# Ten units of a gated feed-forward stage read the moving operand of their matmuls in ten other column orders

## The chip, the cores and the metric

The kernel runs on one core of one Trainium2 chip. The metric is the device time of one execution in microseconds, from the runs of the whole program; details come from one profiled execution.

## The reference: what is computed

One layer of a decoder on 256 tokens of width 2048, all in float32. Three sub-layers, each behind an RMSNorm: a gated feed-forward network with 5632 hidden columns (its result is halved), a mixer of two groups of attention heads, and a second gated network like the first.

```python
def swiglu(x, w_gate, w_up, w_down):
    return (jax.nn.silu(x @ w_gate) * (x @ w_up)) @ w_down

h = h + 0.5 * swiglu(rms_norm(h, norm_ffn1_g[l]), ffn1_w_gate[l], ffn1_w_up[l], ffn1_w_down[l])
...
h = h + o @ w_out[l]
h = h + 0.5 * swiglu(rms_norm(h, norm_ffn2_g[l]), ffn2_w_gate[l], ffn2_w_up[l], ffn2_w_down[l])
```

The 5632 hidden columns of the first network are independent of each other up to the last product, which sums over them. If the columns of gate and up are computed in another order, the result is the same as long as the rows of `w_down` stand in that order too.

## The kernel before

**Products.** Every large product of float32 matrices is made of three matmuls: each operand is split into a high part in float32r and a low part (what the high part left), and `mm3` (L400 to L402) adds high by high, high by low and low by high into one PSUM bank. The stationary operand is a 128 x 128 piece of the activations, the moving operand is a 128 x 512 piece of the weights, and 512 columns of PSUM are written.

**Units.** `ffn` (one call for each feed-forward network) walks the hidden columns in NB = 11 blocks of 512. A *unit* b makes gate and up of a block for all 256 tokens, from eight tiles of weights of 128 x 2048 (four pieces of 512 columns each: two of gate, two of up). A tile is used in one of two ways, which a string names for each unit. "D" is plain: eight products, from the four pieces and two halves of the tokens. "S" is a scheme with seven products, for which VectorE forms sums of the pieces (tile `sums`), so that seven pieces of 512 columns are used. Unit 0 has eight D, unit 1 four D and four S, unit 2 two D and six S, units 3 to 10 one D and seven S: 64, 60, 58 and 57 products.

**Down.** Behind unit b + 1 come the products of block b with its `w_down` rows (`down`, 32 products): the gated block is turned into rows by eight transposes (`turned`, L602) into the tile `hT`, which is the stationary operand there; the moving operand is again 512 columns of weights. The order is in PLAN:

```python
PLAN = [("U", 0)] + [x for b in range(1, NB) for x in (("U", b), ("D", (b - 1,)))][:-1] + [("D", (NB - 2, NB - 1))]
```

**Weights on their way.** A tile of weights comes by one DMA on SP's queue into `raw` (`rawx`, `rawy` are further buffers of the same kind), ScalarE casts it to the high part (`whi`, `whix`, `whiy`), and VectorE subtracts for the low part (`wlo`, `wlox`, `wloy`, L464). The sums of the S scheme are cast and split in the same way. All tiles are 2048 columns wide, and a piece is a run of 512 of them.

**Order.** `Task` objects carry each instruction's engine, cost and needs; `arrange` simulates them with a table of costs and writes out the order of all five engines. In `group` the products of one tile are made, each by `product`, whose `run` calls `mm3` with the views of one piece: `w[1]()` gives the high and the low part's view. `product` and `group` know nothing of the unit's number in the kernel before.

**Arrays.** `_arrays` lays out the inputs on the host ahead of the launch; `by_two` arranges `w_down` for the loads.

Of the kernel before, what the change touches and what calls it, by code (L numbers as in the profile page):

```python
# [36 lines left out]
NB = FF // 512  # L37
# [12 lines left out]
F2_ORDER = [(0, "rawy", F32)] + [(2, "whiy", F32R), (3, "wloy", F32R)] * FREE2 + [(1, "sums", F32)] * NSUM  # L50
F2_ORDER += [(2, "whiy", F32R)] * (NHI - 2 - FREE2) + [(3, "wloy", F32R)] * (NLO - 2 - FREE2) + [(0, "rawy", F32)] * (NRAW - 3)
PAD = 48


C_ID, C_INVF, C_ONE, C_TRI, C_MSK = 0, 128, 160, 288, 416
# [218 lines left out]
def hybrid_layer(ctx: ExitStack, tc: tile.TileContext, a: dict, out: bass.AP):  # L274
# [124 lines left out]
    def mm3(o, shi, slo, mhi, mlo, start, stop, seeded=False):  # L399
        nc.tensor.matmul(o, lhsT=shi, rhs=mhi, start=start, stop=False, skip_group_check=seeded)  # L400
        nc.tensor.matmul(o, lhsT=shi, rhs=mlo, start=False, stop=False, skip_group_check=seeded)  # L401
        return nc.tensor.matmul(o, lhsT=slo, rhs=mhi, start=False, stop=stop, skip_group_check=seeded)  # L402
# [29 lines left out]
    def ffn(pool, u, wgu, wd, slots, banks, rstd, held=None, first=None, lead=None, done=None, out=None):  # L432
# [26 lines left out]
        def bank_of(b):  # L459
            return banks[b["first"].got["bank"][0]]  # L460
# [82 lines left out]
            new = [(ld, -30), (c, 0), (a, 0), (l, 0)] + [(t, 3) for t in (ca, b0, b, cb, ls)]  # L543
            return new, w, {2: [("hi", c), ("lo", l)], 6: [("hi", ca), ("lo", ls)]}

        def product(held, key, stat, w, need):

            t = task("pe", 0.681, None, list(need) + w[0], lag=0.25)
            b = held.setdefault(key, {"first": t})
            if "seed" in b and "last" not in b:  # L550
                t.need.append(b["first"])
            if b["first"] is t:
                t.take = {"bank": 1}
            b["last"] = t

            def run():
                t.made = mm3(bank_of(b), *stat(), *w[1](), start=b["first"] is t, stop=b["last"] is t, seeded="seed" in b)

            t.run = run
            main.append(t)  # L560
            return t

        def group(kind, src, held, stat, need, form=None, pieces=1, last=False, behind=None):

            new, w, free = seven(src) if kind == "S" else added_low(src) if kind == "L" else whole(src, pieces, behind)
            n0 = len(main)
            if kind == "S":
                for i, (key, k, t) in enumerate((
                    ("Q0", 0, 0), ((0, 0), 1, 0), ((0, 1), "f", 0), ("Q1", "f", 3),
                    ("Q3", "f", 2), ("Q2", "f", 1), ((1, 0), 1, 1),  # L570
                )):
                    sh = (lambda t=t: form[1](t)) if k == "f" else (lambda k=k, t=t: stat(k, t))
                    x = product(held, key, sh, w[i], form[0] if k == "f" else need(k))
                    x.give = free.get(i, [])
            else:
                order = [(i, t) for i in range(4) for t in range(NT)]
                if last:
                    order.sort(key=lambda it: it[1])
                for i, t in order:
                    k = (0, 1, 1, 0)[i]  # L580
                    x = product(held, (t, i // 2), lambda k=k, t=t: stat(k, t), w[i], need(k))
                x.give = list(free[3])
            for t, d in new:
                t.due = n0 + d
            return n0
# [65 lines left out]
        forms = {}  # L651
# [44 lines left out]
        def unit(b):  # L696

            kinds, ns = units[b], count[b]
            pair = {"S": iter(sorted(seven_of[:ns])), "D": iter(sorted(seven_of[ns:]))}
            held, hs, sq3 = {}, [], []  # L700
            for n, kind in enumerate(kinds):
                p = next(pair["D" if kind == "L" else kind])
                if b == 0 and first is not None:
                    first[0](p, task, ready)
                if kind == "S" and p not in forms:
                    fresh[p] = len(main)
                    form_of(p, used.get(p, []) + [x for k in (2 * p, 2 * p + 1) for x in ready.get(k, ())], len(main) - 4)
                n0 = group(
                    kind, wgu[b][p], held, lambda k, t, p=p: halves(u(2 * p + k), t), lambda k, p=p: ready.get(2 * p + k, ()),
                    forms.get(p) if kind == "S" else None, (4, 2)[p] if b == 0 and first is not None and p < 2 else 1, n == len(kinds) - 1,  # L710
                )
                used[p] = [main[-1]]
                if b == 0 and first is not None:
                    hs.append(first[1](p, task))
# [11 lines left out]
            if ns:  # L726
                q = task("act", cast(512), None, [held["Q0"]["last"]], due, take={"s": 1, "sq": 2}, give=[("bank", held["Q0"]["first"])])
                x, y = lambda: sq_tile(q, 0), lambda: sq_tile(q, 1)
# [16 lines left out]
                v = [step(up[0], (0, 1), y, ALU.add, [d2], due + 1, False), step(up[1], (1, 1), x, ALU.add, [d4], due + 5, False)]  # L745
            ends = []
            for t in range(NT):
                src = (lambda t=t: s_tile()[:, t, :]) if ns else (lambda t=t: bank_of(R(t, 0)))
                a = task("act", 0.63, lambda t=t, src=src: nc.scalar.activation(
                    s_tile()[:, t, :], src(), AF.Silu, scale=rms[0][:, t : t + 1]  # L750
                ), [g[t] if ns else R(t, 0)["last"]] + rm_need, due + 9 if ns else due + 2 * t, take={"s": 1} if not ns and t == 0 else ())
                if t == 0:
                    a0 = a
                if not ns:
                    a.give.append(("bank", R(t, 0)["first"]))
                src = lambda t=t: bank_of(R(t, 1))
                f = task("dve", 0.66, lambda t=t, src=src: stt(
                    out=s_tile()[:, t, :], in0=src(), scalar=half_rms()[:, t : t + 1], in1=s_tile()[:, t, :], op0=ALU.mult, op1=ALU.mult,
                ), [a, v[t] if ns else R(t, 1)["last"]], due + 9 if ns else due + 2 * t, lag=1.5, psum=True)
# [646 lines left out]
def _arrays(x, positions, norm_ffn1_g, ffn1_w_gate, ffn1_w_up, ffn1_w_down, norm_mix_g, w_in, b_forget,  # L1406
            fox_q_norm_g, fox_k_norm_g, swa_q_norm_g, swa_k_norm_g, swa_sinks, out_norm_fox_g, out_norm_swa_g,
            w_out, norm_ffn2_g, ffn2_w_gate, ffn2_w_up, ffn2_w_down):
    f32 = np.float32
    d = {}  # L1410

    def blocks(w, rows, cols):

        n, m = w.shape
        w = w.reshape(n // P // rows, rows, P, m // cols, cols).transpose(3, 0, 2, 1, 4)
        return w.reshape(m // cols, n // P // rows, P, rows * cols)

    def cols(w):
        return blocks(w, 2, 512)

    def twos(w0, w1):

        x = np.stack([cols(w0).reshape(-1, w0.shape[0] // (2 * P), P, 2, 512), cols(w1).reshape(-1, w1.shape[0] // (2 * P), P, 2, 512)])
        x = np.stack([x[0, ..., 0, :], x[0, ..., 1, :], x[1, ..., 1, :], x[1, ..., 0, :]], -2)
        return x.reshape(*x.shape[:-2], 2048)

    def by_two(w):
        v = w.reshape(w.shape[0], -1, 2, 512)
        return twos(v[:, :, 0].reshape(w.shape[0], -1), v[:, :, 1].reshape(w.shape[0], -1))

    d["wgu1"], d["wd1"] = twos(ffn1_w_gate[0], ffn1_w_up[0]), by_two(ffn1_w_down[0])
    d["wgu2"], d["wd2"] = twos(ffn2_w_gate[0], ffn2_w_up[0]), by_two(ffn2_w_down[0])
    w = w_in[0]
    nf = NH * HD
    d["ws"] = blocks(w[:, 3 * nf :], 2, SWC)
    d["wf"] = np.stack([blocks(w[:, i * nf : (i + 1) * nf], 2, 512) for i in range(3)], 1)
    d["wo"] = np.stack([cols(w_out[0][:nf]), cols(w_out[0][nf:])])
    d["xT"] = x[0].T.reshape(KD // 2, 2, P, SEQ).transpose(0, 2, 1, 3)
    d["x"] = x[0].reshape(NT, P, D)
    d["pos"] = positions[0].reshape(NT, P).T  # L1440

    vec = np.zeros((P, V_END), f32)
    for col, g in (
        (V_G1, norm_ffn1_g), (V_GM, norm_mix_g), (V_G2, norm_ffn2_g), (V_GF, out_norm_fox_g), (V_GS, out_norm_swa_g),
    ):
        n = g.shape[1] // P
        vec[:, col : col + n] = g[0].reshape(n, P).T
    vec[:, V_BF : V_BF + NH] = b_forget[0]
    vec[:, V_SINK : V_SINK + NH] = swa_sinks[0]
    vec[:, V_SQ : V_SQ + HD] = swa_q_norm_g[0]  # L1450
    vec[:, V_SK : V_SK + HD] = swa_k_norm_g[0]
    vec[:HD, V_FQ] = fox_q_norm_g[0]
    vec[:HD, V_FK] = fox_k_norm_g[0]
    vec[HD : HD + 2, V_FQ : V_FK + 1] = 1.0
    d["vec"] = vec

    cst = np.zeros((P, C_END), f32)
    i, j = np.arange(P)[:, None], np.arange(P)[None, :]
    cst[:, C_ID : C_ID + P] = i == j
    cst[:, C_ONE : C_ONE + P] = 1.0  # L1460
    cst[:, C_TRI : C_TRI + P] = i <= j
    cst[:, C_MSK : C_MSK + P] = np.where(j > i, 0.0, NEG)
    for m in (C_MSK + P, C_MSK + 3 * P):
        cst[:, m : m + P] = np.where(j <= i, 0.0, NEG)
    cst[:, C_INVF : C_INVF + 32] = (10000.0 ** (-np.arange(0, HD, 2, dtype=np.float64) / HD)).astype(f32)
    d["cst"] = cst
    return {k: np.ascontiguousarray(v) for k, v in d.items()}
# [17 lines left out]
```

## Time and profile before

| | |
|---|---|
| runs | 1734.42 and 1735.99 us, median 1735.2 |
| profiled execution | 1734.49 us; span of its instructions 1732.7 us |
| granted clock of TensorE | 1.000 |
| TensorE (PE) busy | 1721.5 us, 99% of the span, 7989 matmuls |
| VectorE (DVE) busy | 1557.7 us, 90% |
| ScalarE (ACT) busy | 1161.1 us, 67% |
| DMA | 339.73 MB, mean 196 GB/s |

The span runs from the first to the last instruction of the profiled execution; the execution's own time is 1.8 us longer. Matmuls are pipelined: the next one starts before the last one's end, so that the length of one (0.39 us) is longer than the distance of two starts, and the distance is what counts.

### The profile page before, as it was taken

The page shows a single profiled execution, that of the slowest core. Times are in us where ns is not written, and L with a number is a line of the kernel's source. Part 1 is how long each engine was busy: PE and PEld are TensorE (multiplying, and loading weights), DVE is VectorE, ACT ScalarE, POOL GpSimd, SP SyncE. Part 2 cuts the span into 40 slices and gives each one's busy share as a digit, 9 for nine tenths or more (in the row PEclk, how much of TensorE's full clock was granted, in tenths as well). Part 3 has the DMA queues.
Part 4 walks back from the last instruction along what each step waited for, and adds up shares of the span by engine and source line. Part 5 has one row for each costly group of instructions (what it writes and reads, how often), then busy time and mean ns, then how long its engine had stood idle before and what let it go on. Part 6 is the DMA issues. An engine that isn't in the chain of part 4 may idle for free.

```text
span 1732.7 us, 21114 instructions
## 1 busy us (share of the span) xinstructions
PE 1721.5 (99%) x7989; PEld 1431.7 (83%) x7989; DVE 1557.7 (90%) x1724; ACT 1161.1 (67%) x1416; POOL 106.7 (6%) x40
## 2 busy tenths in 40 slices
PE   9999999999999999999999999999999999999999
PEld 6888888888888888998788888888888888888887
DVE  7999999999999996668777769999999999999994
ACT  6677777767776764555766556667767777776761
POOL 0011001101101100000000000001101101100100
PEclk9999999999999999999999999999999999999999
DMA  9556456556645653574444456446556646655652
GB/s 366 196 215 219 168 202 240 204 182 216 223 172 217 219 205 128 168 212 153 137 145 145 134 202 259 166 174 224 196 189 218 242 160 223 220 186 194 232 194 97
DMA packets 62918, 339.73 MB, mean 196 GB/s; under 512 B 6752, under 2 KB 15456, under 8 KB 29280
## 3 DMA queue, kind: packets, MB, share of 16 engines
q1 hardware_dynamic: 62208, 337.18, 54.8%
q8 instruction: 62, 1.02, 0.2%
q0 software_dynamic: 320, 1.05, 0.1%
q14 instruction: 40, 0.33, 0.1%
q10 hardware_dynamic: 288, 0.16, 0.0%
HBM read 336.27 MB, written 2.10 MB: 195 GB/s over the span
## 4 chain that ended last, share of the span: by engine, by line
PE 97%; DVE 1%; DMA 1%; ACT 1%; SPq 0%; issue 0%; DVEq 0%; ACTq 0%
PE acc L401 25%; PE acc L400 25%; PE acc L402 25%; PE sm L401 6%; PE sm L402 6%; PE sm L400 6%; PE acc L602 1%; PE sm L1131 1%; PE sc L1320 1%; DMA rawx<-in_wgu 1%; PE sm L1137 1%; PE sm L602 0%; PE sm L1299 0%; DVE wloy L464 0%; PE sc L1245 0%; PE sm L1138 0%
## 5 line engine op out<-in xcount | busy, mean ns | idle before, releaser
L400 PE MATMUL acc<-whi,u 128*128 128x512 f32 (+1 forms) x659 | 251.5, 383 | 1.1 <-DVE s L1095 0.9
L401 PE MATMUL acc<-wlo,u 128*128 128x512 f32 (+1 forms) x659 | 251.2, 382 | 0.8 <-DVE wlo L464 0.8
L402 PE MATMUL acc<-whi,u 128*128 128x512 f32 (+1 forms) x659 | 249.9, 381 | 0.0
L317 DVE TENSOR_TENSOR wlo<-raw,whi 128x1024 fp32r<-128x1024 f32 (+1 forms) x112 | 128.8, 1154 | 74.0 <-ACT whi L316 73.5
L316 ACT CAST whi<-raw 128x1024 fp32r<-128x1024 f32 (+1 forms) x112 | 111.0, 991 | 96.3 <-PE acc L402 87.0
L400 PEld LDWEIGHTS acc<-whi,u 128*128 128x128 f32 x659 | 123.7, 188 | 23.5 <-DVE s L1095 1.3
L401 PEld LDWEIGHTS acc<-wlo,u 128*128 128x128 f32 x659 | 123.7, 188 | 21.7 <-DVE wlo L464 1.1
L402 PEld LDWEIGHTS acc<-whi,u 128*128 128x128 f32 x659 | 123.6, 188 | 21.1 <-issue 0.8
L464 DVE TENSOR_TENSOR wlo<-sums,whi 128x2048 fp32r<-128x2048 f32 x53 | 121.2, 2287 | 3.2 <-ACT whi L519 2.3
L464 DVE TENSOR_TENSOR wlo<-raw,whi 128x1536 fp32r<-128x1536 f32 (+3 forms) x57 | 107.3, 1884 | 8.1 <-ACT whi L490 7.1
L830 ACT COPY h<-acc 128x512 f32<-128x512 f32 (+1 forms) x115 | 64.5, 567 | 69.3 <-PE acc L402 69.1
L464 DVE TENSOR_TENSOR wloy<-sums,whiy 128x2048 fp32r<-128x2048 f32 x41 | 93.7, 2286 | 2.4 <-ACT whiy L519 1.7
L464 DVE TENSOR_TENSOR wlox<-rawx,whix 128x2048 fp32r<-128x2048 f32 (+1 forms) x42 | 86.4, 2058 | 6.2 <-ACT whix L490 5.1
L464 DVE TENSOR_TENSOR wlox<-sums,whix 128x2048 fp32r<-128x2048 f32 x39 | 89.2, 2286 | 0.7
L538 DVE TENSOR_TENSOR sums<-sums,raw 128x512 f32<-128x512 f32 x130 | 87.8, 687 | 1.3
L400 PE MATMUL acc<-whi,hT 128*128 128x512 f32 x216 | 84.8, 392 | 0.0
L402 PE MATMUL acc<-whi,hT 128*128 128x512 f32 x216 | 84.1, 389 | 0.0
L401 PE MATMUL acc<-wlo,hT 128*128 128x512 f32 x216 | 84.1, 389 | 0.0
L464 DVE TENSOR_TENSOR wloy<-raw,whiy 128x2048 fp32r<-128x2048 f32 (+1 forms) x39 | 80.1, 2053 | 3.7 <-ACT whiy L514 1.8
L401 PE MATMUL acc<-wlox,u 128*128 128x512 f32 x205 | 79.9, 390 | 0.5 <-DVE wlox L464 0.5
L401 PE MATMUL acc<-wloy,u 128*128 128x512 f32 x205 | 80.0, 390 | 0.4 <-DVE wloy L464 0.3
L400 PE MATMUL acc<-whix,u 128*128 128x512 f32 x205 | 79.8, 390 | 0.0
(344 smaller groups left out, 4776.9 us busy)
## 6 DMA issues: line engine op xcount, KB each, us to landing
raw<-in_wgu SPq DMA_DIRECT2D x86, 1024.0 KB, 4.8
rawx<-in_wgu SPq DMA_DIRECT2D x44, 1024.0 KB, 4.9
raw<-in_wd SPq DMA_DIRECT2D x44, 1024.0 KB, 4.8
rawy<-in_wgu SPq DMA_DIRECT2D x44, 1024.0 KB, 4.8
raw<-in_wf SPq DMA_DIRECT2D x48, 512.0 KB, 3.3
rawx<-in_wd SPq DMA_DIRECT2D x22, 1024.0 KB, 4.8
rawy<-in_wd SPq DMA_DIRECT2D x22, 1024.0 KB, 4.8
raw<-in_wo SPq DMA_DIRECT2D x32, 512.0 KB, 3.3
```

The lines of the kernel that those rows point to most:

```text
L316: nc.scalar.copy(hi, src)
L317: nc.vector.tensor_tensor(out=lo, in0=src, in1=hi.bitcast(F32), op=ALU.subtract)
L400: nc.tensor.matmul(o, lhsT=shi, rhs=mhi, start=start, stop=False, skip_group_check=seeded)
L401: nc.tensor.matmul(o, lhsT=shi, rhs=mlo, start=False, stop=False, skip_group_check=seeded)
L402: return nc.tensor.matmul(o, lhsT=slo, rhs=mhi, start=False, stop=stop, skip_group_check=seeded)
L464: tt(out=o_, in0=a, in1=f32(b), op=ALU.subtract)
L538: tt(out=s[n + 2], in0=s[2 * n], in1=cols_of(raw())[r], op=ALU.add)
L602: nc.tensor.transpose(bt[:, j * SEQ + t * P : j * SEQ + (t + 1) * P], src()[:, t, m], ident)
L830: nc.scalar.copy(o_, src)
L1131: nc.tensor.transpose(bt[:, j * P : (j + 1) * P], src[:, j, :], ident)
L1137: nc.tensor.matmul(bo[rows, c0 : c0 + SEQ], lhsT=vals(0, j), rhs=p0[:, j, :], start=True, stop=False)
L1320: nc.tensor.matmul(o_, lhsT=qk_[:, 0, j, blk * P : (blk + 1) * P], rhs=qk_[:, 1, j, 0:nk], start=True, stop=True)
```

## The change

A table LINES names an order for each of the units 1 to 10 of the first feed-forward stage. Where a product of such a unit reads its piece of 512 columns, high or low, `in_lines` gives it a view with the same 512 columns in another order. The numbers of products, tiles, loads, casts and subtractions stay, and the instructions of all engines stand in the same order as before. Unit 0, the down products and the second network read as before. On the host the 512 rows of `w_down` of each block are put into the block's order.

```diff
+LINES = {
+    1: "(a b) -> a b:32", 2: "(a x b) -> x a b:2,32", 3: "(x a b) -> a x b:2,32", 4: "(x a b) -> a x b:2,16",
+    5: "(x a b) -> a x b:2,4", 6: "(x a b) -> a x b:2,1", 7: "(a x b) -> x a b:2,16", 8: "(x a b) -> a x b:4,32",
+    9: "(x a b) -> a x b:4,16", 10: "(a x b) -> x a b:2,1",
+}
+
+
+def in_lines(b, t):
+
+    if b not in LINES:
+        return t
...
+    return t.rearrange("p %s -> p %s" % (left, right), **by)
...
-        def product(held, key, stat, w, need):
+        def product(held, key, stat, w, need, line=None):
...
-                t.made = mm3(bank_of(b), *stat(), *w[1](), start=b["first"] is t, stop=b["last"] is t, seeded="seed" in b)
+                t.made = mm3(bank_of(b), *stat(), *(in_lines(line, x) for x in w[1]()), start=b["first"] is t, stop=b["last"] is t, seeded="seed" in b)
...
-                    forms.get(p) if kind == "S" else None, (4, 2)[p] if b == 0 and first is not None and p < 2 else 1, n == len(kinds) - 1,
+                    forms.get(p) if kind == "S" else None, (4, 2)[p] if b == 0 and first is not None and p < 2 else 1, n == len(kinds) - 1, line=b if first is not None else None,
...
-    d["wgu1"], d["wd1"] = twos(ffn1_w_gate[0], ffn1_w_up[0]), by_two(ffn1_w_down[0])
+    d["wgu1"], d["wd1"] = twos(ffn1_w_gate[0], ffn1_w_up[0]), by_two(
+        np.concatenate([in_lines(b, r) for b, r in enumerate(ffn1_w_down[0].reshape(NB, 512, -1))])
+    )
```

An entry reads as follows. The 512 columns are cut into x parts or x alternating pieces with runs of b columns. "(x a b) -> a x b:2,16" takes 16 columns from the first half, 16 from the second, the next 16 from the first, and so on. "(a x b) -> x a b:2,16" takes the 1st, 3rd, 5th run of 16 and so on, then the 2nd, 4th, 6th. As the matmul's operand, each is (step, count) from the slowest to the fastest:

| unit | order | steps and counts | matmuls |
|---|---|---|---|
| 1 | as before | (1, 512) | 180 |
| 2 | every second run of 32, then the others | (32, 2) (64, 8) (1, 32) | 174 |
| 3 | runs of 32, from two halves in turn | (32, 8) (256, 2) (1, 32) | 171 |
| 4 | runs of 16, from two halves in turn | (16, 16) (256, 2) (1, 16) | 171 |
| 5 | runs of 4, from two halves in turn | (4, 64) (256, 2) (1, 4) | 171 |
| 6 | single columns, from two halves in turn | (1, 256) (256, 2) | 171 |
| 7 | every second run of 16, then the others | (16, 2) (32, 16) (1, 16) | 171 |
| 8 | runs of 32, from four quarters in turn | (32, 4) (128, 4) (1, 32) | 171 |
| 9 | runs of 16, from four quarters in turn | (16, 8) (128, 4) (1, 16) | 171 |
| 10 | even columns, then odd columns | (1, 2) (2, 256) | 171 |

More of the change, by code (lines that the diff above doesn't have):

```diff
@@ L52 @@
 PAD = 48
+LINES = {
[3 rows of a table added]
+}
+def in_lines(b, t):
+    if b not in LINES:
+        return t
+    how, by = LINES[b].split(":")
+    by = dict(zip("xb" if "x" in how else "b", map(int, by.split(","))))
+    if isinstance(t, np.ndarray):
+        left, right = how.split(" -> ")
+        names = left.strip("()").split()
+        n = {k: by.get(k) for k in names}
+        n["a"] = t.shape[0] // int(np.prod([v for v in n.values() if v]))
+        v = t.reshape([n[k] for k in names] + list(t.shape[1:]))
+        v = v.transpose([names.index(k) for k in right.split()] + list(range(len(names), v.ndim)))
+        return v.reshape(t.shape)
+    left, right = how.split(" -> ")
+    return t.rearrange("p %s -> p %s" % (left, right), **by)
 C_ID, C_INVF, C_ONE, C_TRI, C_MSK = 0, 128, 160, 288, 416
@@ L561, in product, with group @@
             return t
-        def group(kind, src, held, stat, need, form=None, pieces=1, last=False, behind=None):
+        def group(kind, src, held, stat, need, form=None, pieces=1, last=False, behind=None, line=None):
             new, w, free = seven(src) if kind == "S" else added_low(src) if kind == "L" else whole(src, pieces, behind)
@@ L572, in group @@
                     sh = (lambda t=t: form[1](t)) if k == "f" else (lambda k=k, t=t: stat(k, t))
-                    x = product(held, key, sh, w[i], form[0] if k == "f" else need(k))
+                    x = product(held, key, sh, w[i], form[0] if k == "f" else need(k), line)
                     x.give = free.get(i, [])
@@ L580, in group @@
                     k = (0, 1, 1, 0)[i]
-                    x = product(held, (t, i // 2), lambda k=k, t=t: stat(k, t), w[i], need(k))
+                    x = product(held, (t, i // 2), lambda k=k, t=t: stat(k, t), w[i], need(k), line)
                 x.give = list(free[3])
```

## The prediction

> **What bounds the kernel now.** I read the page's first two parts and the granted clock, then the chain that ended last, then a table of stretches in the stage that is edited, and last single instructions in order of time, because the edit changes how one kind of instruction reads its operand and nothing else.
>
> ```profile
> span 1732.7 us, 21114 instructions
> PE 1721.5 (99%) x7989; PEld 1431.7 (83%) x7989; DVE 1557.7 (90%) x1724; ACT 1161.1 (67%) x1416; POOL 106.7 (6%) x40
> PEclk9999999999999999999999999999999999999999
> PE 97%; DVE 1%; DMA 1%; ACT 1%; SPq 0%; issue 0%; DVEq 0%; ACTq 0%
> PE acc L401 25%; PE acc L400 25%; PE acc L402 25%; PE sm L401 6%; PE sm L402 6%; PE sm L400 6%; PE acc L602 1%; PE sm L1131 1%; PE sc L1320 1%; DMA rawx<-in_wgu 1%; PE sm L1137 1%; PE sm L602 0%; PE sm L1299 0%; DVE wloy L464 0%; PE sc L1245 0%; PE sm L1138 0%
> ```
>
> The reader should see that PE is busy in 99% of the span and that 97% of the chain is PE, nearly all of it the three matmuls of `mm3` (L400, L401, L402), which are exactly the instructions that the edit touches. The clock is full throughout.
>
> Busy time on PE is modelled, so I take the true pace from the repeating pattern. These are the rows of the chain that ended last for the turning of the rows, which comes once in each unit, and the table of stretches for two unit periods in the first stage (columns: length, then busy time of PE, PEld, DVE, ACT, POOL with their counts, clock, DMA share, GB/s):
>
> ```profile
> 410.60 0.87 PE acc L602 x8
> 472.01 0.87 PE acc L602 x8
> 533.43 0.87 PE acc L602 x8
> 348.50:410.00 61.50, 61.50 (x278) 50.99 (x277) 60.59 (x52) 44.76 (x47) 5.20 (x1) 1.00 0.58 206
> 410.00:471.50 61.50, 61.50 (x277) 51.03 (x276) 60.59 (x52) 44.55 (x48) 5.22 (x1) 1.00 0.57 205
> ```
>
> A period is 61.41 us (472.01 - 410.60). It holds 57 products of a unit and 32 of the down half, at three matmuls each 267, and eight transposes that take 0.87. So one matmul costs (61.41 - 0.87) / 267 = **0.2267 us**, and PE is never idle in the stretch. VectorE comes right behind: 60.59 of 61.50.
>
> Single matmuls give the same pace (timeline; start, length, engine, line):
>
> ```profile
> 420.17 0.39 PE L400 MATMUL acc<-whix,hT 128*128 128x512 f32 x1
> 420.39 0.39 PE L401 MATMUL acc<-wlox,hT 128*128 128x512 f32 x1
> ...
> 421.30 0.39 PE L402 MATMUL acc<-whix,hT 128*128 128x512 f32 x1
> 421.53 0.39 PE L400 MATMUL acc<-whix,hT 128*128 128x512 f32 x1
> ```
>
> From 420.17 to 421.53 there are six starts in 1.36 us, 0.2267 each. For 512 columns that is 0.443 ns for each column. PE streams columns; it waits for nobody.
>
> Two other kinds of matmul in this trace say what the 0.443 consists of:
>
> ```profile
> 700.26 0.33 PE L402 MATMUL acc<-whi,u 128*128 128x388 f32 x1
> 700.43 0.34 PE L400 MATMUL acc<-whi,u 128*128 128x388 f32 x1
> 700.61 0.33 PE L401 MATMUL acc<-wlo,u 128*128 128x388 f32 x1
> 700.78 0.34 PE L402 MATMUL acc<-whi,u 128*128 128x388 f32 x1
> 876.25 1.89 PE L1320 MATMUL sc<-aug 66*128 66x256 f32 x8
> L1320 PE MATMUL sc<-aug 66*128 66x256 f32 x32 | 7.7, 379 | 0.0
> ```
>
> 388 columns start 0.17 and 0.18 us apart in turn (0.17 / 388 = 0.44 ns, the short ones), so the pace goes with the number of columns, and there is little fixed cost in a matmul that a longer read could hide in. In the last two rows eight matmuls of plain float32 take 1.89 us with a last one of 0.379, so they start (1.89 - 0.379) / 7 = 0.216 us apart for 256 columns: 0.84 ns a column. The float32r kind that the edit touches therefore draws its moving operand about twice as fast as the plain kind, 4 bytes for each partition every 0.443 ns. I read that as a port without much to spare, and this is the choice on which the forecast rests.
>
> **The change part by part.** No instruction is added, removed or moved: counts and orders on all five engines are the same, the matmuls still write 512 columns in a row to PSUM, and the down rows are laid out on the host before the launch, so their loads have the same sizes. Terms of zero are therefore the loads, the casts, the subtractions, the products of the down half and everything behind the first stage; they cost nothing as long as they hide under PE, and where PE becomes slower they have more cover, not less (a weight load of 188 ns lies under a matmul of 227 ns):
>
> ```profile
> L400 PEld LDWEIGHTS acc<-whi,u 128*128 128x128 f32 x659 | 123.7, 188 | 23.5 <-DVE s L1095 1.3
> ```
>
> What remains is how long a matmul takes that reads its 512 columns in another order. The trace of before has no such read: each matmul reads columns in a row. So every unit is bounded from both sides. Unit 1's order is the old one (two nested runs that join into one): 0. The other nine units have these reads, each for 171 matmuls (174 in unit 2), and a doubling of one unit is worth 171 x 0.2267 = **38.8 us**:
>
> - Units 2, 3 and 8: runs of 32 columns. Units 4, 7 and 9: runs of 16. Unit 5: runs of 4. Below, zero: a run's columns still come in a row, and the old matmuls jump to another tile every 512 columns with no gap in their starts. Above, one lost slot of 0.443 ns for each run. There are 16 x 174 + (16 + 32 + 128 + 32 + 16 + 32) x 171 = 46560 runs, 20.6 us. I take 0, being nearest to the rows (a matmul's start is a jump too, and costs under what the starts resolve).
> - Unit 6: runs of 1; columns alternate between two places 256 columns apart, so no column has its neighbour beside it. Below, 0, if the port addresses each column by itself. Above, four times the time, 3 x 38.8 = 116.3, if the port brings four neighbours at a time and each such visit lasts as long as four columns now.
> - Unit 10: even columns, then odd ones. Two are a step of two apart, so half of what lies between is wasted. Below, 0; above, 38.8, for a port that brings two or four neighbours at a time and throws half away.
>
> I take a port that brings **two neighbouring columns in one go**, at 2 x 0.443 ns. It fits a port whose visits come at the pace of plain float32 (0.84 ns a column) and which serves float32r with two columns to a visit (2 x 0.443 = 0.89 ns), and it stands between the ends. Then a lone column costs a whole go: units 6 and 10 double, all others stay. The sum is 2 x 38.8 = +77.5 us. The cover is nil: PE is on the chain in every moment of the stage, so all of it reaches the end. The profiled execution took 1734.49 us, 1.8 more than its span of 1732.7, and lies 0.7 below the median of 1735.2. So 1734.5 + 77.5 = **1812 us**.
>
> [...]
>
> **The rivals.**
>
> *Only lone columns far apart pay.* A read that keeps the last place open would serve unit 10 at the old pace and lose a slot only where the next column lies far off: unit 6 doubles, +38.8, 1773.3. If each broken run loses a slot as well, the upper end of the runs comes in, +20.6, 1793.9. For it: the old matmuls show no cost at a jump, so it must be small. Against it: unit 10 would draw from twice as many bytes in the same time. [...]
>
> *Four neighbours at a time.* Four columns are 16 bytes; if a visit to such a group takes 4 x 0.443 = 1.77 ns whatever is taken from it, unit 6 needs 512 visits where it had 128, four times its time, and unit 10 twice. Unit 5, whose runs of four fill a group each, stays. 116.3 + 38.8 = +155.1, 1889.6. For it: the pace in strict proportion to columns, as of a read that is saturated. Against: nothing in the trace marks a step of four.
>
> *The order is free.* This is the one on the other side, not slower: PE's port forms an address for each column, and the 0.443 ns are the array's own pace. Price 0, 1734.5; it decides if the starts in units 6 and 10 stay 0.2267 apart. For it: jumps between tiles cost nothing visible. Against: float32r is the kind that draws bytes fastest here, so that a read order which costs nothing anywhere would be luck. Nor can an order that reads more quickly bring much: VectorE fills 60.59 of 61.50 us in a period, so nine units give back at most 9 x 0.91 = 8.2 us, 1726. That the change doesn't do what it says is not a case of its own: the columns come out in the order in which they are read, in a free layout of the same length.
>
> *Groups wider than four.* With 16 columns to a visit, unit 5 would take four times, unit 6 sixteen times and unit 10 twice as long: (3 + 15 + 1) x 38.8 = +737. I only keep a small chance for it and its like.
>
> **How the numbers follow.** Pairs (1812): 0.28. Groups of four (1890): 0.24. Far columns only (1773, or 1794 with the runs): 0.22. Free (1735, with small gains and losses): 0.15. Above all of these: 0.11. The point is the likeliest, 1812. Leaving out the free case and the top would leave out 0.26, so the range goes down to it, 1733 to 1892, and leaves out the top alone. Slower and no change together hold most of the chance; the slower cases by themselves reach from 1773 to 1890. Two per cent of 1735 (about what a measurement of this kernel can tell from no change) is 34.7 us: pairs, groups of four and the top lie above it, as do most of the far-column cases, though unit 6 alone lies only 4 us above. So slower 0.78, within 2% 0.20, faster 0.02.
>
> **What the profile after would show.** Starts 0.2267 us apart in units 1 to 5 and 7 to 9, and 0.453 in units 6 and 10, whose periods grow from 61.4 to about 100 us, with VectorE idle for the difference; the second feed-forward stage as before. If unit 10's starts stay, the far-column rival is right; if unit 6's are 0.907, the groups of four; if both stay, the free order. Wrong in every case would be a cost in units 2 to 4 or 7 to 9, whose runs are 16 columns and more, or a wait for VectorE or a load inside the slower units.

## The result, and the profile after

The changed kernel takes **1785.24 us** (1785.19 to 1785.29) against 1735.2: +50.0 us, a ratio of 1.0288 with a 95% interval of 1.0244 to 1.0333. It is slower by more than 2%, as forecast, and lies inside the range, 27 us under the point of 1812. The mechanism of the forecast, though, is only half right, and the half that fails is the more useful one.

The page of the changed kernel (first lines, clock, and the chain that ended last; L425 to L427 are the former L400 to L402):

```profile
span 1783.5 us, 21114 instructions
PE 1773.2 (99%) x7989; PEld 1437.3 (81%) x7989; DVE 1559.5 (87%) x1724; ACT 1164.1 (65%) x1416; POOL 104.0 (6%) x40
PEclk9999999999999999999999999999999999999999
PE 96%; DVE 2%; DMA 1%; issue 1%; ACT 0%; SPq 0%; DVEq 0%; ACTq 0%
PE acc L426 24%; PE acc L425 24%; PE acc L427 24%; PE sm L426 6%; PE sm L425 6%; PE sm L427 6%; PE acc L627 1%; DVE wlox L489 1%; PE sm L1156 1%; PE sc L1345 1%; DMA rawx<-in_wgu 1%; PE sm L1162 1%; PE sm L627 0%; PE sm L1324 0%; DVE wlo L489 0%
```

The span grew by 50.8 us, PE's busy time by 51.7, and VectorE and ScalarE work as much as before. PE is still the chain. So the matmuls became longer, and the clock did not change (granted 1.000 in both).

How long they became is read in the timeline, unit by unit. Unit 4 (runs of 16), unit 6 (single columns from two halves in turn) and unit 10 (even, then odd columns):

```profile
259.80 0.40 PE L425 MATMUL acc<-whix,u 128*128 128x512 f32 x1
...
261.96 0.40 PE L425 MATMUL sm<-whix,fu 128*128 128x512 f32 x1
380.24 0.38 PE L425 MATMUL sm<-whix,fu 128*128 128x512 f32 x1
...
382.40 0.38 PE L426 MATMUL sm<-wlox,u 128*128 128x512 f32 x1
639.44 0.63 PE L425 MATMUL acc<-whix,u 128*128 128x512 f32 x1
639.89 0.64 PE L426 MATMUL acc<-wlox,u 128*128 128x512 f32 x1
...
642.62 0.63 PE L426 MATMUL sm<-wlox,u 128*128 128x512 f32 x1
```

Nine starts in 2.16 us are 0.240 us each in unit 4. Ten starts in 2.16 us are **0.216** in unit 6: quicker than before. Seven starts in 3.18 us are **0.454** in unit 10. The table of stretches shows unit 10 from the other side (the first row is the same unit in the kernel before):

```profile
609.85:648.40 38.55, 38.55 (x172) 31.92 (x171) 37.84 (x30) 27.75 (x23) 0.00 (x0) 1.00 0.53 190
621.00:700.00 79.00, 79.00 (x179) 36.68 (x178) 41.45 (x33) 29.71 (x25) 0.00 (x0) 1.00 0.30 109
```

PE is busy for all 79 us, with 179 matmuls where 348 would fit at the old pace. VectorE, which was busy for 37.84 of the 38.55 us that this unit took before, has 41.45 of 79, and the DMA share falls from 0.53 to 0.30. No other engine keeps PE waiting; PE alone is slow.

Distances of starts (medians over a unit's matmuls in the trace, means where two values alternate), and what they add:

| unit | order | us | added to 0.2267, us in all |
|---|---|---|---|
| 1 | in a row | 0.227 | 0 |
| 2, 3 | runs of 32 | 0.237 | +1.7 and +1.7 |
| 4, 7 | runs of 16 | 0.240 | +2.3 and +2.3 |
| 5 | runs of 4, two halves | 0.250 | +4.0 |
| 6 | single columns, two halves | 0.216 | -1.8 |
| 8 | runs of 32, four quarters | 0.233 | +1.1 |
| 9 | runs of 16, four quarters | 0.231 | +0.8 |
| 10 | even, then odd columns | 0.453 | +38.7 |

The sum is +50.8 us, the whole growth of the span. Unit 10 alone makes three quarters of it. (Waits of PE inside the units cancel: by its starts it lost about 0.5 us in unit 3 before, and as much in unit 6 now.)

In unit 6, the one that became quicker, the chain changes hands. These are two of its pieces there and the stretch around them:

```profile
389.09 2.28 DVE wlox L489
399.90 4.53 DVE wlox L489 x3
349.00:411.00 62.00, 61.73 (x284) 52.55 (x283) 60.55 (x52) 44.17 (x48) 6.50 (x1) 1.00 0.56 202
```

From 375 to 409 us the chain runs mostly over VectorE, and PE, which had no idle time around this unit before (61.50 of 61.50 us from 348.50 to 410.00), is idle for 0.27 of 62 us. So VectorE (60.55 of these 62.00 us busy) is the next bound, and it lies close.

### The profile page after: what moved, and what is told of

The parts are those of the page before. It is cut to its first block, busy times and chain, and to the rows that moved or that the text cites. A ratio compares the mean times of both kernels' runs of the same rounds, so it can differ in the third digit from the quotient of the medians.

```text
span 1783.5 us, 21114 instructions
## 1 busy us (share of the span) xinstructions
PE 1773.2 (99%) x7989; PEld 1437.3 (81%) x7989; DVE 1559.5 (87%) x1724; ACT 1164.1 (65%) x1416; POOL 104.0 (6%) x40
## 4 chain that ended last, share of the span: by engine, by line
PE 96%; DVE 2%; DMA 1%; issue 1%; ACT 0%; SPq 0%; DVEq 0%; ACTq 0%
PE acc L426 24%; PE acc L425 24%; PE acc L427 24%; PE sm L426 6%; PE sm L425 6%; PE sm L427 6%; PE acc L627 1%; DVE wlox L489 1%; PE sm L1156 1%; PE sc L1345 1%; DMA rawx<-in_wgu 1%; PE sm L1162 1%; PE sm L627 0%; PE sm L1324 0%; DVE wlo L489 0%
## 5 line engine op out<-in xcount | busy, mean ns | idle before, releaser
L425 PE MATMUL acc<-whi,u 128*128 128x512 f32 (+1 forms) x659 | 254.9, 388 | 0.9 <-DVE s L1120 0.9
L427 PE MATMUL acc<-whi,u 128*128 128x512 f32 (+1 forms) x659 | 253.3, 386 | 0.0
L425 PEld LDWEIGHTS acc<-whi,u 128*128 128x128 f32 x659 | 124.2, 189 | 25.3 <-issue 2.8
L427 PEld LDWEIGHTS acc<-whi,u 128*128 128x128 f32 x659 | 124.0, 188 | 23.6 <-issue 3.0
L426 PE MATMUL acc<-wlox,u 128*128 128x512 f32 x205 | 85.4, 417 | 0.6 <-DVE wlox L489 0.6
L425 PE MATMUL acc<-whix,u 128*128 128x512 f32 x205 | 85.4, 416 | 0.3 <-DVE s L758 0.3
L427 PE MATMUL acc<-whix,u 128*128 128x512 f32 x205 | 85.3, 416 | 0.0
L425 PE MATMUL acc<-whi,hT 128*128 128x512 f32 x216 | 84.8, 393 | 0.0
L427 PE MATMUL acc<-whi,hT 128*128 128x512 f32 x216 | 84.1, 389 | 0.0
```

## The experiments

The edits of the LINES table are shown as the orders; the rest of those kernels is the changed kernel, with `in_lines` able to read an order with one more letter y.

**Steps and streams (one execution).** Unit 6 has a step of 256 columns and unit 10 a step of 2, and they come out on opposite sides. This kernel fills in the steps between.

```diff
+    1: "(x a b) -> a x b:4,1",
+    2: "(x a b) -> a x b:8,1",
+    3: "(x a b) -> a x b:16,1",
+    4: "(x a b) -> a x b:32,1",
+    5: "(x a b) -> a x b:64,1",
+    6: "(x a b) -> a x b:128,1",
+    7: "(x a b) -> a x b:2,2",
+    8: "(x a b) -> a x b:2,8",
+    9: "(y x a b) -> y a x b:2,2,1",
+    10: "(y x a b) -> y a x b:16,2,1",
```

> The changed kernel with ten other orders in units 1 to 10. Units 1 to 6 read single columns a fixed step apart and come back for the next: steps of 128, 64, 32, 16, 8 and 4 columns (4, 8, 16, 32, 64 and 128 streams of columns in turn; unit 6 of the changed kernel was a step of 256, unit 10 a step of 2). Unit 7 takes pairs, unit 8 runs of 8 from two halves in turn; unit 9 takes single columns from two streams 128 apart, unit 10 from two streams 16 apart. Theory A, open places: the port keeps a few fetched stretches open, and two streams let one fetch hide behind the other. Then steps of 128 stay near 0.216 us, the time grows where there are more streams than open places, up to several times 0.2267 for steps of 16 to 4 columns, and units 7, 9 and 10 are at 0.216 to 0.227. Theory B, pairs and banks: two columns are read at a time, free if they share a place or lie in different banks, double if they lie in one bank. Then only the distance of consecutive columns counts: each unit is either near 0.216 or near 0.44, never above, and unit 10 tells whether 16 columns are far enough. My forecast's theory (a lone column costs double) would have all of units 1 to 6, 9 and 10 at 0.45; unit 6 of the changed kernel speaks against it already.

The kernel takes 1954.94 us. Distances of starts: steps of 128, 64, 32, 16, 8 and 4 columns take 0.284, 0.487, 0.435, 0.433, 0.431 and 0.460 us; pairs from two halves 0.340, runs of 8 from two halves 0.243; two streams 128 apart and two streams 16 apart 0.216 both. Timeline rows of unit 4 (step 16) and of unit 10 (two streams 16 apart):

```profile
359.65 0.61 PE L434 MATMUL acc<-whix,u 128*128 128x512 f32 x1
...
362.25 0.61 PE L434 MATMUL acc<-whix,fu 128*128 128x512 f32 x1
844.63 0.38 PE L434 MATMUL acc<-whi,u 128*128 128x512 f32 x1
...
846.79 0.38 PE L432 MATMUL acc<-whix,u 128*128 128x512 f32 x1
```

Six starts in 2.60 us are 0.433; ten in 2.16 are 0.216. In both units each column lies 16 columns from the one ahead of it or behind it, and one takes twice the time of the other. So the distance of consecutive columns does not decide, and theory B falls, although its ceiling of about twice the time holds (0.487 us at most). Theory A's sizes fall too: it had up to several times 0.2267 for steps of 16 to 4, where about twice was measured, near 0.216 for steps of 128, which take 0.284, and 0.216 to 0.227 for pairs, which take 0.340. Its idea that one fetch can hide behind another does not fall by this, and is not shown by it. What fits these times, all but the 0.284 and the 0.340, is my estimate from them, a model: a port in which **two readers take columns in turn**: the first has the 1st, 3rd, 5th column of the order, the second the 2nd, 4th, 6th. In the model each reader walks along a row of neighbours with two streams (0.216), and steps by 4 with one stream of step 2 (0.453).

**Unit 10's order alone (four executions).** The table is cut to its last entry.

> The changed kernel with unit 10's order (even columns, then odd ones) alone; units 1 to 9 read columns in a row. If the starts of the changed kernel add up, unit 10 costs 171 x (0.453 - 0.227) = +38.7 us: 1774, ratio 1.022. Rival: part of the changed kernel's gain and loss comes from something that the units share (waits at their borders, VectorE): then this run differs by more than 3 us from 1774.

1772.99 us (ratio 1.0226, interval 1.0211 to 1.0242): 39.0 more than the 1733.98 of the kernel before, which ran beside it, and 1 us from the expected 1774. The starts add up, and unit 10's loss is its own: no part of it is shared with other units.

**Two readers, put to the test (one execution).**

```diff
+    1: "(y x a b) -> y a x b:64,2,1",
+    2: "(y x a b) -> y a x b:128,2,1",
+    3: "(y x a b) -> y a x b:32,2,1",
+    4: "(x a y) -> y a x:2,2",
+    5: "(x a y) -> y a x:4,2",
+    6: "(y x a b) -> y a x b:32,4,1",
+    7: "(y x a b) -> y a x b:16,8,1",
+    8: "(a x b) -> x a b:2,2",
+    9: "(a x b) -> x a b:2,4",
+    10: "(a x b) -> x a b:2,8",
```

> The changed kernel with ten further orders in units 1 to 10. Theory L, two readers: the columns are served in turn by two readers (1st, 3rd, 5th column and 2nd, 4th, 6th), each holds a line of four neighbouring columns (16 bytes) or two such lines, keeps the full pace if it takes at least two columns from a line before it leaves it, and costs double if only one. Theory W, wasted bytes: whoever reads, what counts is how many lines are fetched for a column, so that any order that skips every second column doubles. Per matmul, L and W: unit 1, single columns from two streams 4 apart: 0.216, 0.216. Unit 2, two streams 2 apart (columns 0, 2, 1, 3): both readers share a line as in a plain row, 0.227, 0.227. Unit 3, two streams 8 apart: 0.216, 0.216. Unit 4, even columns of both halves in turn, then the odd ones: each reader takes two of four columns of a line, 0.216 to 0.227; W 0.45. Unit 5, every fourth column of both halves in turn: one for each line, 0.43 to 0.46; W 0.45 or more. Unit 6, four streams 4 apart: as four streams 128 apart, 0.284; unit 7, eight streams 4 apart: as eight streams 64 apart, 0.43 to 0.49. Unit 8, pairs with gaps of a pair (0, 1, 4, 5, ...): each reader one of each line, 0.45; a theory of pairs fetched together has 0.227. Unit 9, fours with gaps of four: each reader two from a line, 0.227 to 0.25; W 0.227. Unit 10, eights with gaps of eight: 0.227 to 0.245.

The kernel takes 1861.46 us. Distances of starts in units 1 to 10: 0.216, 0.227, 0.216, 0.227, 0.452, 0.268, 0.480, 0.452, 0.231, 0.233. Nine values fall on or into theory L's numbers; unit 6 is 0.016 under (its number and unit 7's had been carried over from the steps and streams, not worked out from the theory). Timeline rows of unit 4 (even columns of two halves in turn) and unit 8 (pairs with gaps of a pair):

```profile
249.62 0.39 PE L434 MATMUL acc<-whi,fu 128*128 128x512 f32 x1
...
251.89 0.39 PE L432 MATMUL acc<-whi,u 128*128 128x512 f32 x1
599.53 0.63 PE L433 MATMUL sm<-wlox,fu 128*128 128x512 f32 x1
...
602.25 0.64 PE L433 MATMUL acc<-wlox,u 128*128 128x512 f32 x1
```

Ten starts in 2.27 us against six in 2.72. Unit 4 reads every second column, as unit 10 of the changed kernel does, but from two places in turn, so that in theory L each reader steps by 2 and not by 4: the doubling is gone, 0.453 to 0.227. That excludes theory W, for as many columns are passed over. Unit 8 takes its columns in whole pairs, and doubles (0.452), as theory L has it, where each reader steps by 4; that excludes the pairs of my forecast.

A rival of the two readers stands, and it was not run. Take a single reader that holds two groups of four neighbouring columns and, when it has to fetch one, fetches the next column's group in the same time if that is another one. Counted over all orders of the three kernels, it needs as many fetching steps as the busier of two readers that hold one group each: 64 in the units at 0.216, 128 in those at 0.227 to 0.250, 256 in those at 0.43 to 0.49. The one exception is pairs from two halves (128 against 256), whose 0.340 neither gives; four streams (0.284 and 0.268) have 256 in both, and fit neither. An order that visits groups as A, B, B, A and then goes on to fresh ones (columns 0, 4, 5, 1, 8, 12, 13, 9 and so on) would tell: by the same count I estimate about 0.45 us with two readers, about 0.227 with this one. What the two share is what the runs show: the time is about twice (0.43 to 0.49 us) where each column lies in another group of four than the last but one, and not (0.216 to 0.250) where two takes or more come from a group in turn, with pairs from two halves (0.340) and four streams (0.284 and 0.268) in between.

**The quick order everywhere (four executions).** If two streams read at 0.216, the weights can be laid out on the host so that two streams come out in natural order, and nothing else need change.

```diff
+def turns(t):
+    return t.rearrange("p (x a) -> p a x", x=2)
...
-                t.made = mm3(bank_of(b), *stat(), *w[1](), start=b["first"] is t, stop=b["last"] is t, seeded="seed" in b)
+                t.made = mm3(bank_of(b), *stat(), *(turns(x) for x in w[1]()), start=b["first"] is t, stop=b["last"] is t, seeded="seed" in b)
...
-                    acc[t][:, :width], u(kk)[:, 0, ts_], u(kk)[:, 1, ts_], hi[:, m], lo[:, m],
+                    acc[t][:, :width], u(kk)[:, 0, ts_], u(kk)[:, 1, ts_], turns(hi[:, m]), turns(lo[:, m]),
...
-        w = w.reshape(n // P // rows, rows, P, m // cols, cols).transpose(3, 0, 2, 1, 4)
+        w = w.reshape(n // P // rows, rows, P, m // cols, cols // 2, 2).transpose(3, 0, 2, 1, 5, 4)
```

> The kernel before, with unit 6's order (single columns from two halves in turn) in all three-matmul products of the whole kernel, and the weights' columns laid out on the host so that they come out in natural order. Theory: a matmul of 512 columns takes 0.216 instead of 0.2267 us. If PE alone bounds, some 6900 matmuls save 10.7 ns each, 74 us: 1661. If VectorE is the next bound (60.6 us busy in a period of 61.4), the seventeen or so periods with seven-product tiles can only go to about 60.6 to 61, 0.4 to 0.8 us each, while the mixer's products and the first and last blocks keep their gain of about 10 to 15 us: 1705 to 1720. I expect the second, 1712.

**1692.42 us**, ratio 0.9761 (0.9746 to 0.9775). The page's chain, the table of stretches (500 us of the second network), and two turnings of the rows one period apart:

```profile
DVE 57%; PE 30%; issue 11%; DMA 1%; ACT 1%; SPq 0%; DVEq 0%; ACTq 0%
1100.00:1600.00 500.00, 494.21 (x2282) 422.07 (x2281) 497.14 (x435) 365.84 (x402) 52.93 (x8) 1.00 0.59 209
342.18 0.38 PE L606 MATMUL sm<-cst,s 128*128 128x128 f32 x2
402.72 0.38 PE L606 MATMUL acc<-cst,s 128*128 128x128 f32 x2
```

VectorE has taken over the chain, with 497.14 of 500 us busy: the period of a unit goes from 61.41 only to 60.54 us (402.72 - 342.18), as the second case of the expectation had it. The total is 20 us under the expected 1712, because outside those periods I had guessed 10 to 15 us, and there was more: from the last turning of the first network to the first of the second, mostly the mixer, 370.3 us became 353.2, which is 17.1 alone.

**The same with less work for VectorE (four executions).**

```diff
-UNITS = [["D" * 8, x, "DSSSSSSD"] + ["SSSSSSSD"] * (NB - 3) for x in ("DDSSDSSD", "DSSDSSSD")]
+UNITS = [["D" * 8, x, "DSSSSSSD"] + ["DSSSSSSD"] * (NB - 3) for x in ("DDSSDSSD", "DSSDSSSD")]
...
-            t = task("pe", 0.681, None, list(need) + w[0], lag=0.25)
+            t = task("pe", 0.648, None, list(need) + w[0], lag=0.25)
```

> As the run before, and in units 3 to 10 of both networks one more tile is done plainly (six tiles of seven products instead of seven, 58 products instead of 57), which takes about 4 us of VectorE's work out of a period; the planner's cost of a product is 0.648 instead of 0.681 us. If VectorE bounds the run before, this one is quicker although it has three matmuls more in each unit: 270 x 0.216 + 0.87 = 59.2 us a period, 2.2 less than before, about 17 periods, and some 15 us in the rest: 1680 to 1690. If VectorE was not the bound, it is slower than the run before by 16 x 0.65 = 10 us.

**1668.15 us**, ratio 0.962 (0.9604 to 0.9636): 65.8 us less than the kernel before, and the best version of this study.

```profile
PE 91%; DVE 6%; issue 1%; DMA 1%; ACT 1%; SPq 0%; DVEq 0%; ACTq 0%
1100.00:1600.00 500.00, 500.00 (x2350) 438.78 (x2349) 476.31 (x405) 368.57 (x389) 37.47 (x8) 1.00 0.58 211
339.78 0.38 PE L606 MATMUL sm<-cst,s 128*128 128x128 f32 x2
398.93 0.38 PE L606 MATMUL acc<-cst,s 128*128 128x128 f32 x2
```

PE has the chain again and is never idle in these 500 us, VectorE has 5% to spare, and the period is 59.15 us (398.93 - 339.78), against 59.2 expected. The total is 12 us under the expected 1680, again from the parts outside the periods.

**Fewer seven-product tiles alone (four executions).** Only the UNITS line of the last diff, columns in a row.

> The kernel before, with six instead of seven tiles of the seven-product kind in units 3 to 10 of both networks, and columns read in a row as before. 58 products instead of 57: 270 x 0.2267 + 0.87 = 62.1 us a period, 0.68 more in each of 16 units: 1734.0 + 10.9 = 1745, ratio 1.006. It shows how much of the second gain comes from the read order alone. Rival: VectorE's load already cost PE something that the periods don't show; then it is no slower than the kernel before.

1746.05 us, ratio 1.0067 (1.005 to 1.0084), 11.7 more than 1734.31. So the plan pays only together with the order: by itself it loses 11.7 us, on top of the order it gains 24.3 (1692.42 to 1668.15), where the order had moved the bound to VectorE. The two steps are not quite the same edit: the one on top of the order also lowers the planner's cost of a product to 0.648, and what that alone is worth was not run.

## Why the prediction was right or wrong

**The bound, and that all of it reaches the end: right.** The span grew by the sum of the starts, 50.8 us, and PE stayed the chain with 96%. VectorE's slack did grow in the slow unit (41.45 of 79.00 us busy, against 37.84 of 38.55 before). Only in the quicker unit 6 did the chain pass to VectorE (from 375 to 409 us).

**Unit 10: right in size, by the wrong mechanism.** +38.7 us against 38.8, and that agreement is luck. The forecast had two neighbouring columns brought in one go and one thrown away. The pairs with gaps (unit 8 of the test of two readers) throw nothing of a pair away and take 0.452 all the same, and the even columns from two places do and take 0.227.

**Unit 6: wrong, and the step that failed is "a lone column costs a whole go".** -1.8 us against +38.8. I argued from what lies beside a column in the order; what the times of these runs go with, most of all, is what lies two places further on in the order: in unit 10 (0.453) a column four further on, in unit 6 (0.216) the neighbour. By the model of two readers, each of them there takes four columns in a row from each group of four. I had taken "no column has its neighbour beside it" for the worst order, and it is the best one found.

**The runs: mis-sized at zero.** +13.9 us in seven units, inside the bounds of 0 to 20.6. I had put them at nothing because the old matmuls' jumps from tile to tile leave no gap in their starts (0.2267 each); no row of before has a jump inside a matmul, and there it does cost: the 16 runs in unit 2 cost 9.9 ns, 0.62 for each. It isn't one price: a run costs 0.42 ns in unit 4, 0.18 in unit 5 and 0.14 in unit 9, and what sets it stays open. With unit 6 the two errors come to -40.6 + 13.9 = -26.7, which is the distance from 1812 to 1785. That the two errors have opposite signs is luck too.

**A port without much to spare: right as far as the starts tell, and it was the useful part.** The 0.2267 us of a plain row are not the array's own pace; two streams give 0.216. That is the case that the forecast dismissed with "nor can an order that reads more quickly bring much". For the nine units alone that holds (VectorE bounds at 60.54 us a period), but it counted neither the rest of the kernel nor a plan that gives VectorE less; with these two the whole gain came to 65.8 us. That a port sets the time stays my estimate: what the runs show is that the time goes with the order of reading, from 0.216 to 0.487 us for the same 512 columns.

**The rivals.** "Only lone columns far apart pay" and "four at a time" had unit 6 as the dear one and fall with it (0.216); "the order is free" falls with unit 10 (0.453); groups wider than four fall with unit 5, which would have taken four times 0.2267 and takes 0.250. How many columns a matmul as a whole takes from a group of four neighbours before it moves on does not give the times: unit 10 takes two and has 0.453, a row takes four and has 0.2267, and unit 6 takes one at a time and has 0.216. Counted over every second column, as for each of two readers, the takes go with the times: where such a reader steps by 2 columns (two takes from a group, unit 4 of the test of two readers) a matmul takes 0.227, where it steps by 4 (one take, unit 10, and units 5 and 8 of that test) 0.452 to 0.453.

What stays open: two readers are a model that foretold the numbers of its test, unit 6 apart, not a thing seen, and the single reader with two fetches at a time fits as well. Neither gives the sizes of the cases between: pairs from two halves (0.340), four streams (0.284 when 128 apart, 0.268 when 4 apart), or eight (0.487 and 0.480).

## What to carry to other kernels

Where PE bounds, try the order in which it reads the moving operand: it costs no instruction (21114 before and after), and a host layout gives the natural order back. A float32r operand stored with its even columns ahead of its odd ones, and read from the two halves in turn, took 4.7% less time here (0.216 against 0.2267 us a matmul), while reading every second column in a row doubled the time (0.453). Ask then which engine is next (here VectorE, 60.59 of 61.50 us busy) and re-balance the plan, which was worth more than half of the first gain again (24.3 us after 41.6).

## What the runs showed of the hardware that was not expected

- A matmul with a float32r moving operand of 512 columns takes 0.2267 us when the columns stand in a row and 0.216 when they come in turn from two streams 4, 8, 16, 128 or 256 columns apart; streams 2 apart give 0.227 again.
- An order in which each column lies 4 or more columns from the last but one, and the four neighbours of a group are not visited again soon, takes 0.43 to 0.49 us (steps of 2, 4, 8, 16, 32 and 64 columns, every fourth column of two halves, pairs with gaps, eight streams 4 apart); nothing tried took more.
- Breaks of a row cost something in themselves: runs of 32, 16 and 4 columns, with gaps or from several places in turn, take 0.233 to 0.237, 0.231 to 0.240 and 0.231 to 0.250 us.
- With 388 columns, as in the mixer, two streams bring the starts from 0.172 and 0.182 in turn to a steady 0.164 us (the trace of the quick order with six tiles).
